# Seven-product down projection, with low parts made by an adding transfer, in a float32 decoder layer on one core

## The chip, the core and the metric

The kernel is one program on one NeuronCore of a Trainium2 chip. The metric is the device time of one execution in microseconds. Engines are named as the profile names them: PE multiplies matrices (PEld is its weight load), DVE and ACT work on vectors, POOL is GpSimd, SP issues the transfers.

## The reference, cut to what matters

The layer ends in a gated MLP. With 512 tokens, 1024 model features and 2816 inner features, the part that is changed is

```
u = causal_dwconv(h @ w_up, ffn_conv_w, ffn_conv_b)      # (512, 5632)
u_gate, u_val = split(u, 2)
x = x + gate_f * ((silu(u_gate) * u_val) @ w_down)       # (512, 2816) @ (2816, 1024)
```

All data are float32. Everything before it (norms, attention, recurrence, merge, output projection) is as it was.

## The kernel before

Features lie on the partitions, tokens along the free axis. A matrix product runs on PE in a rounded type (F32R) that loses low bits, so each float32 operand is kept as two rounded parts, high and low, and `mm3` issues three matmuls per 128x128 block of weights: high by high, high by low, low by high (line 384). `mm` (line 181) is the helper in which every matmul is recorded (L187 in the profile).

Weights come as a stream of chunks of 128x1024, that is eight blocks. A chunk is loaded into one of three `raw` tiles by SP, `split` (line 375) copies it into a `hi` tile on ACT (or, if ACT is behind in the plan, on DVE) and subtracts on DVE into a `lo` tile. There are three of each: a chunk's split waits until PE is done with the chunk three before it, and a load waits until the split of the chunk three before it is done (`stream_to`, `next_chunk`, lines 536 and 548).

The up projection has 44 output tiles of 128 features, one chunk each. For a tile, `conv3` reads the PSUM bank (one ACT and two DVE instructions), and for a pair of tiles `act_task` applies SiLU, multiplies, and splits the product into a pair of rounded slots, `AH[i]` and `AL[i]`; there are 22 of them.

The down projection (lines 1395 to 1407) has 8 output tiles `j`, one after the other, each a sum over the 22 inner tiles `k`. A matmul covers 512 tokens; the last tile goes in two halves of 256. One DVE instruction per tile adds the gated result to the residual `X2[j]`, and SP stores it.

The program is not issued in the order in which it is written. Each operation goes onto a list with a price, and `flush` (line 272) plans it: for each engine it takes, among the next few of its list (`WINDOW`, 160 for PE), the operation that can start first by the planner's own prices, the older one on a tie, and issues it there. The chip's queues then run in exactly this order, whatever the real times are. There is one `flush`, at the end. Tokens' data lie in `pair` tiles (20 slots of 512 columns) and 60 `rslot` tiles.

Of the kernel before, what the change touches and what calls it, by code (L numbers as in the profile page):

```python
# [49 lines left out]
SLACK, NEAR, BACKLOG, LIMIT = 1.2, 2, 8, 2  # L50

FLY, FIRST = 4, 5

# [30 lines left out]
class Emitter:  # L84
# [187 lines left out]
    def flush(self):  # L272
# [23 lines left out]
        end = [None] * len(ops)  # L296
        table = None
# [39 lines left out]
        while left:  # L337
            e = min((x for x in choice if choice[x]), key=lambda x: choice[x][1])
            late, t, i = choice[e]
            op = ops[i]  # L340
            if e == "act" and self.switches(op[5], table):
                t += 1.3
                table = op[5]
            c = pe_cost(t, i) if e == "pe" else op[1]
            free[e] = end[i] = t + c
            if e == "dma":
# [28 lines left out]
    def split(self, hi, lo, x):  # L375

        if self.in_order is None:
            self.act(hi, x, AF.Copy)
        else:
            self.cast(hi.r if isinstance(hi, Buf) else hi, x)  # L380
        h = hi.ap if isinstance(hi, Buf) else hi.bitcast(F32)
        self.tt(lo.r if isinstance(lo, Buf) else lo, x, h, OP.subtract)

    def mm3(self, out, wh, wl, xh, xl, first, last):

# [86 lines left out]
def hybrid_trunk_kernel(ctx: ExitStack, tc: tile.TileContext, xT, vec, cvec, cst, chot, rel, wm, w8, wz, wgate, wbr,  # L472
                        wout, wup, wdn, outT):
    nc = tc.nc
    sb = ctx.enter_context(tc.tile_pool(name="sb", bufs=1))
    pp = ctx.enter_context(tc.tile_pool(name="pp", bufs=1, space=bass.MemoryType.PSUM))
    dr = ctx.enter_context(tc.tile_pool(name="dr", bufs=1, space=bass.MemoryType.DRAM))
    ctx.enter_context(tc.manual_schedule())

    NF, NR = 20, 60  # L480
    slots = []
    for i in range(NF // 2):
        w = sb.tile([128, 1024], F32, name=f"pair{i}")[:]
        slots += [Buf(w[:, :512], w), Buf(w[:, 512:], w)]
    rslots = [Buf(sb.tile([128, 512], F32R, name=f"rslot{i}")[:]) for i in range(NR)]
    banks = [Buf(pp.tile([128, 512], F32, name=f"bank{i}")[:]) for i in range(8)]
    E = Emitter(nc, banks, slots, rslots)
# [6 lines left out]
    halves = (slice(0, 256), slice(256, 512))  # L494
# [21 lines left out]


    c8 = sb.tile([128, 8], F32, name="c8")[:]
    E.dma(c8, cvec, 4, act=True)
    E.dma(CS, cst, 66, act=True)  # L520
    X = [E.slot() for _ in range(KT)]
# [5 lines left out]


    plan = []

    class Stream:
        i = 0
# [3 lines left out]
    def stream_to(n_load, n_split):  # L536
        while Stream.loaded < min(n_load, len(plan)):
            i = Stream.loaded
            src = plan[i]
            E.dma(raws[i % 3][:, :src.shape[-1]], src, 4 * 128 * src.shape[-1] / 1024)  # L540
            Stream.loaded += 1
        while Stream.split < min(n_split, len(plan)):
            i = Stream.split
            n = plan[i].shape[-1]
            E.split(his[i % 3][:, :n], los[i % 3][:, :n], raws[i % 3][:, :n])
# [12 lines left out]

    MODV = sb.tile([128, 32], F32, name="modv")[:]

    def rsqrt(out, ssq, n, inv):

# [43 lines left out]

    ident = CS[:, C_ID:C_ID + 128]
    cp = E.pair()
    gq = sb.tile([128, 2], F32, name="gq")[:]
    relt = sb.tile([32, 16], F32, name="relt")[:]  # L610
    junk = sb.tile([128, 1], F32, name="junk")[:]
    wmp = {}

    def load_wm(f, i):
# [24 lines left out]
    for k in range(KT):  # L639
        t = sq[0 if k == 0 else 3 if k == 7 else 1 + k % 2]  # L640
# [74 lines left out]
    for f in range(KT):  # L715
# [12 lines left out]
        wh, wl = his[f % 3], los[f % 3]  # L728
# [272 lines left out]
    plan.extend(wdn[i] for i in range(22))  # L1001


    mod = {}
# [25 lines left out]
        E.drop(*c2)  # L1030

    nsp = sb.tile([128, 8], F32, name="nsp")[:]

    def nsp_task():
        a, t, s, s2, acc = small(8), small(8), small(8), small(8), small(8)
# [164 lines left out]
    for at, (kind, t) in enumerate(order):  # L1202
# [5 lines left out]
        if kind in ("g", "h"):  # L1208
            b = "g h".index(kind)
# [57 lines left out]
        wh, wl = next_chunk()  # L1267
        z = E.bank()
# [10 lines left out]
    X2 = XR  # L1279
# [83 lines left out]
    def act_task(i, u, w):  # L1363
        yield Need(aps=(u.ap,))
        E.act(u.ap, u.ap, AF.Silu)
        yield Need(aps=(u.ap, w.ap), rslots=2)
        E.tt(u.ap, u.ap, w.ap, OP.mult)
        h, l = E.rslot(), E.rslot()
        E.split(h, l, u.ap)
        E.drop(u, w)  # L1370
        AH.append(h)
        AL.append(l)

    first = []
    E.finish(tn[0])
    for i in range(FIRST):
        wh, wl = next_chunk()
# [1 line left out]
        project(first[i].ap, wh, wl, halves[0], Fh, Fl)  # L1379
    E.finish(tn[1])  # L1380
    E.drop(acc)
    for i in range(44):
# [8 lines left out]
        if i % 2:  # L1391
            ta = E.spawn(act_task(i // 2, uc.pop(i - 1), uc.pop(i)))
    E.finish(ta, t_mod)
    E.drop(*Fh, *Fl)
    dn = []
    for j in range(8):
        for cs in halves if j == 7 else (slice(0, S),):
            z = E.bank()
            for k in range(FT):
                n = j * FT + k  # L1400
                if n // 8 == len(dn):
                    dn.append(next_chunk())
                wh, wl = dn[n // 8]
                E.mm3(z.ap[:, cs], blk(wh, n % 8), blk(wl, n % 8), AH[k].r[:, cs], AL[k].r[:, cs], k == 0, k == FT - 1)
            E.stt(X2[j].ap[:, cs], z.ap[:, cs], mod["gate_f"][:, j:j + 1], X2[j].ap[:, cs], OP.mult, OP.add)
            E.drop(z)
            E.dma(outT[j][:, cs], X2[j].ap[:, cs])
    E.flush()


# [92 lines left out]
```

## Time and profile before

| | |
|---|---|
| three runs, median (lowest to highest) | 904.74 us (904.73 to 904.83) |
| the profiled execution, device time | 904.71 us |
| its span, first to last instruction | 902.9 us |
| PE busy | 893.7 us |
| DVE busy | 629.7 us |
| ACT busy | 473.5 us |
| POOL busy | 1.8 us |
| granted clock of TensorE | 1.000 of full speed |

The span is 1.8 us shorter than the device time; what lies outside it is not in the trace. Matmuls overlap each other in the profile, so the pace of PE is read from the distance between starts and not from the duration of one.

### The profile page before, as it was taken

To read this page: it belongs to the slowest core of one execution; us is meant where nothing else is said; L and a number is where in the kernel's file an instruction comes from. 1 tells how busy PE (TensorE), PEld (TensorE's weight loads), DVE (VectorE), ACT (ScalarE), POOL (GpSimd) and SP (SyncE) were. 2 spreads that over 40 slices of the span, in tenths; PEclk is the share of its full clock that TensorE was granted. 3 is DMA by queue.
4 is the path that set the end of the run, shared out by engine and by line. 5 is a ranking of instruction groups with operands and counts; after the bars stand their busy time and mean duration, and the time that the engine had idled before them with its cause. 6 is when DMAs were issued, how large, how long until landed. Compare 5 with 4: busy or idle time off the path is not lost.

```text
span 902.9 us, 12516 instructions
## 1 busy us (share of the span) xinstructions
PE 893.7 (99%) x4748; PEld 771.9 (85%) x4748; DVE 629.7 (70%) x1131; ACT 473.5 (52%) x759; POOL 1.8 (0%) x15
## 2 busy tenths in 40 slices
PE   7999999999999999999999999999999999999998
PEld 6889989889888888878888999888888888888888
DVE  7989998997876875887676889765666665522321
ACT  5376768985875897732223566544444444321110
POOL 0000000000000000000000000000000000000000
PEclk9999999999999999999999999999999999999999
DMA  9934432452245244685667655333222233333320
GB/s 329 336 117 116 159 82 92 140 159 87 86 160 170 78 144 145 186 289 203 238 230 277 209 184 166 120 106 101 95 94 94 94 98 107 98 117 105 117 82 24
DMA packets 44286, 131.70 MB, mean 146 GB/s; under 512 B 5393, under 2 KB 6937, under 8 KB 44226
## 3 DMA queue, kind: packets, MB, share of 16 engines
q1 hardware_dynamic: 43938, 130.83, 43.6%
q8 instruction: 37, 0.61, 0.3%
q14 instruction: 23, 0.19, 0.1%
q10 hardware_dynamic: 288, 0.07, 0.0%
HBM read 122.46 MB, written 5.80 MB: 142 GB/s over the span
## 4 chain that ended last, share of the span: by engine, by line
PE 93%; ACT 3%; DVE 3%; issue 1%; DMA 0%; POOLq 0%; POOL 0%; DVEq 0%; ACTq 0%
PE bank L187 90%; PE bank L191 2%; ACT pair L213 1%; ACT L213 1%; DVE pair L240 1%; DVE pair L246 0%; DMA c<-in_cvec_dram 0%; DVE pair L243 0%; ACT rslot L213 0%; DVE lo L240 0%; ACT hi L213 0%; DVE rslot L240 0%; DVE pair L258 0%; DVE rslot L243 0%; DVE hi L230 0%
## 5 line engine op out<-in xcount | busy, mean ns | idle before, releaser
L187 PE MATMUL bank<-rslot,hi 128*128 128x512 f32 (+1 forms) x2332 | 657.1, 367 | 0.4 <-ACT rslot L213 0.4
L187 PEld LDWEIGHTS bank<-rslot,hi 128*128 128x128 f32 x2332 | 419.6, 189 | 70.4 <-ACT rslot L213 0.8
L187 PE MATMUL bank<-rslot,lo 128*128 128x512 f32 (+1 forms) x1166 | 427.0, 367 | 0.0
L240 DVE TENSOR_TENSOR lo<-raw,hi 128x1024 fp32r<-128x1024 f32 (+1 forms) x169 | 197.6, 1171 | 151.4 <-ACT hi L213 150.2
L213 ACT ACTIVATE hi<-raw 128x1024 fp32r<-128x1024 f32 (+1 forms) x153 | 156.8, 1025 | 188.5 <-PE bank L187 162.0
L187 PEld LDWEIGHTS bank<-rslot,lo 128*128 128x128 f32 x1166 | 219.8, 189 | 35.7
L187 PE MATMUL bank<-hi,rslot 128*128 128x256 f32 (+1 forms) x448 | 92.0, 315 | 0.3 <-ACT rslot L213 0.3
L243 DVE SCALAR_TENSOR_TENSOR pair<-bank,V,pair 128x511 f32<-128x511 f32 (+2 forms) x112 | 83.5, 746 | 2.8 <-ACT pair L213 1.1
L187 PEld LDWEIGHTS bank<-hi,rslot 128*128 128x128 f32 x448 | 74.3, 190 | 6.6 <-issue 0.9
L213 ACT ACTIVATE rslot<-pair 128x512 fp32r<-128x512 f32 (+2 forms) x60 | 37.2, 622 | 75.8 <-DVE pair L240 71.7
L246 DVE CUSTOM_DVE_ANT_0 pair<-pair,pair,V 128x1024 f32<-128x1024 f32 x48 | 61.1, 1278 | 10.8 <-DMA pair<-in_wm_dram 10.8
L213 ACT ACTIVATE pair<-bank,V 128x512 f32<-128x512 f32 (+1 forms) x84 | 61.6, 733 | 4.7 <-PE bank L187 4.0
L213 ACT ACTIVATE pair<-bank 128x512 f32<-128x512 f32 (+3 forms) x76 | 43.3, 604 | 39.1 <-PE bank L187 38.6
L187 PE MATMUL bank<-lo,rslot 128*128 128x256 f32 (+1 forms) x224 | 62.5, 315 | 0.0
L213 ACT ACTIVATE pair<-pair 128x512 f32<-128x512 f32 (+1 forms) x59 | 33.5, 569 | 46.1 <-DVE pair L243 44.8
L240 DVE TENSOR_TENSOR rslot<-pair,rslot 128x512 fp32r<-128x512 f32 (+2 forms) x67 | 45.4, 679 | 15.1 <-ACT rslot L213 14.7
L240 DVE TENSOR_TENSOR pair<-pair,pair 128x512 f32<-128x512 f32 (+1 forms) x72 | 45.6, 635 | 13.2 <-ACT pair L213 8.3
L213 ACT ACT_TABLE_LOAD x37 | 47.5, 1283 | 6.1 <-PE bank L187 3.8
L187 PE MATMUL bank<-rslot,rslot 128*128 128x256 f32 (+3 forms) x288 | 48.7, 309 | 0.0
L187 PEld LDWEIGHTS bank<-rslot,rslot 128*128 128x128 f32 x288 | 43.4, 189 | 4.7 <-DVE rslot L240 0.8
L213 ACT ACTIVATE pair<-pair,small 128x256 f32<-128x256 f32 (+3 forms) x78 | 40.4, 528 | 10.5 <-DVE small L234 9.4
L187 PEld LDWEIGHTS bank<-lo,rslot 128*128 128x128 f32 x224 | 42.7, 190 | 2.6
(79 smaller groups left out, 410.3 us busy)
## 6 DMA issues: line engine op xcount, KB each, us to landing
raw<-in_wz_dram SPq DMA_DIRECT2D x50, 512.0 KB, 3.4
raw<-in_wup_dram SPq DMA_DIRECT2D x49, 512.0 KB, 3.3
pair<-in_wm_dram SPq DMA_DIRECT2D x48, 512.0 KB, 5.0
raw<-in_wdn_dram SPq DMA_DIRECT2D x22, 512.0 KB, 3.3
raw<-in_wout_dram SPq DMA_DIRECT2D x16, 512.0 KB, 3.3
pair<-in_xT_dram SPq DMA_DIRECT2D x16, 256.0 KB, 5.0
raw<-in_w_dram SPq DMA_DIRECT2D x8, 512.0 KB, 6.1
raw<-in_wbr_dram SPq DMA_DIRECT2D x16, 256.0 KB, 3.0
```

Source lines behind the costliest of these rows:

```text
L187: self._go("pe", cost, [out], [lhsT, rhs], lambda: self.nc.tensor.matmul(out, lhsT, rhs, start=start, stop=stop), rows=lhsT.shape[0] / 128)
L191: self._go("pe", 0.107, [out], [in_, ident], lambda: self.nc.tensor.transpose(out, in_, ident))
L213: self._go("act", c, outs, ins, lambda: self.nc.scalar.activation(out, in_, func, scale=scale, **kw), "tanh" if func == AF.Tanh else t)
L240: self._dve([out], [a, b], lambda: self.nc.vector.tensor_tensor(out, a, b, op=op))
L243: self._dve([out], [a, s, b], lambda: self.nc.vector.scalar_tensor_tensor(out, a, s, b, op0=op0, op1=op1))
L246: self._dve([out, accum], [a, b, s], lambda: self.nc.vector.tensor_tensor_reduce(out, a, b, 1.0, s, op0, op1, accum_out=accum))
```

## The change

Output tiles go in four pairs. The first pair is computed as before, but both tiles side by side, in chunks of four inner tiles. For each of the other three pairs, the first 14 of the 22 inner tiles go as seven pairs of inner tiles by Strassen's scheme: a 2x2 block product (two output tiles, two inner tiles, two halves of the tokens) by seven products of 256 tokens in place of eight. The remaining 8 inner tiles go as before, in two chunks.

The sums of weight blocks are made by three DVE additions per chunk ahead of its split, which then covers 896 columns; the four differences of activations per pair of inner tiles are made by DVE in `act_task`, stored to DRAM, and read back, split and kept as `TH`, `TL` during the first pair of output tiles. To have room, the residual is stored to DRAM during the up projection, the plan is flushed ahead of the down projection, and the pool of `pair` tiles is closed and a smaller one opened in its place. For the two plain chunks of each of the three pairs the low part is not subtracted on DVE: ACT writes the high part and its negative, and a transfer issued by POOL adds the raw chunk onto the latter. The planner prices that transfer at 4.0 us from issue to use.

```
+    def split_add(self, hi, lo, x):
+        self.act(hi, x, AF.Copy)
+        self.act(lo, hi.bitcast(F32), AF.Copy, scale=-1.0)
+        self._go("pool", 1.0, [lo], [x], lambda: self.nc.gpsimd.dma_start(lo, x, accum_op=OP.add), table=4.0)
...
             if i in sevens:
+                E.tt(w[:, 512:768].rearrange("p (a n) -> p a n", a=2), w[:, None, 0:128].to_broadcast([128, 2, 128]),
+                     w[:, 128:384].rearrange("p (a n) -> p a n", a=2), OP.add)
+                E.tt(w[:, 768:896], w[:, 512:640], w[:, 256:384], OP.add)
+                E.tt(w[:, 896:1024], w[:, 768:896], w[:, 384:512], OP.add)
+                w = w[:, 128:]
...
+            (E.split_add if i in added else E.split)(his[i % 3][:, :n], los[i % 3][:, :n], w)
...
+        E.tt(t4[0], e.ap[:, a], e.ap[:, b], OP.subtract)
+        E.stt(t4[1], t4[0], -1.0, u.ap[:, b], OP.mult, OP.subtract)
+        E.tt(t4[2], u.ap[:, b], e.ap[:, b], OP.subtract)
+        E.stt(t4[3], t4[1], -1.0, u.ap[:, a], OP.mult, OP.subtract)
+        E.dma(d_t[i // 2], t[0].whole, 512)
...
+    E.flush()
+    first_pool.close()
+    E.slots = take_slots(zp, 8, "z")
...
+        def plain():
+            zs = [E.bank() for _ in range(3 if jp == 3 else 2)]
+            for ks in rest if jp else every:
+                wh, wl = next_chunk()
...
+                for (j, z, cs), k in seq:
+                    n = j * len(ks) + k - ks.start
+                    E.mm3(zs[z].ap[:, cs], blk(wh, n), blk(wl, n), AH[k].r[:, cs], AL[k].r[:, cs], k == (2 * SEVEN if jp else 0),
+                          k == FT - 1)
...
+        def seven():
+            b = [E.bank() for _ in range(4)]
+            for q in range(SEVEN):
+                wh, wl = next_chunk()
...
+                for n, x, cs, z, zc in ((1, e, a, 0, a), (2, o, a, 1, a), (6, o, c, 1, c), (5, t[1], None, 0, c),
+                                        (3, t[0], None, 2, a), (4, t[2], None, 2, c), (0, t[3], None, 3, a)):
+                    E.mm3(b[z].ap[:, zc], blk(wh, n), blk(wl, n), xh, xl, f, l)
+            y, y2, u, w = E.slot(), E.slot(), E.slot(), E.slot()
+            E.act(y.ap[:, a], b[0].ap[:, a], AF.Copy)
+            E.act(w.ap[:, c], b[2].ap[:, a], AF.Copy)
+            E.tt(u.ap[:, a], y.ap[:, a], b[0].ap[:, c], OP.add)
+            E.tt(w.ap[:, a], u.ap[:, a], b[2].ap[:, c], OP.add)
+            E.tt(y.ap[:, c], u.ap[:, a], w.ap[:, c], OP.add)
+            E.tt(y.ap, y.ap, b[1].ap, OP.add)
+            E.stt(xs[0].ap, y.ap, mod["gate_f"][:, j0:j0 + 1], xs[0].ap, OP.mult, OP.add)
+            E.tt(y2.ap[:, a], w.ap[:, a], b[3].ap[:, a], OP.add)
+            E.tt(y2.ap[:, c], w.ap[:, a], w.ap[:, c], OP.add)
+            E.stt(xs[1].ap, y2.ap, ngate[:, j1:j1 + 1], xs[1].ap, OP.mult, OP.add)
...
+        if jp == 0:
+            t_combos = E.spawn(combos())
+            out = plain()
+            E.finish(t_combos)
+        else:
+            seven()
+            out = plain()
```

In the last pair the plain part of its second tile goes in halves of 256, as the last tile did before.

## Rows read from the trace of the kernel before

**Rows 1.** The page, part 1: busy us (share of span), instructions.

```profile
PE 893.7 (99%) x4748; PEld 771.9 (85%) x4748; DVE 629.7 (70%) x1131; ACT 473.5 (52%) x759; POOL 1.8 (0%) x15
```

**Rows 2.** The chain that ended last, 770 us on: start, us, what.

```profile
769.90 129.86 PE bank L187 x635
899.76 0.02 issue
```

**Rows 3.** Groups by form, 779.2 us on: busy us, mean ns, idle before, releaser.

```profile
L187 PE MATMUL bank<-rslot,hi 128*128 128x512 f32 x308 | 94.9, 389 | 0.0
...
L187 PE MATMUL bank<-rslot,lo 128*128 128x512 f32 x154 | 59.9, 389 | 0.0
...
L240 DVE TENSOR_TENSOR lo<-raw,hi 128x1024 fp32r<-128x1024 f32 x20 | 24.5, 1226 | 66.3 <-ACT hi L213 66.2
L213 ACT ACTIVATE hi<-raw 128x1024 fp32r<-128x1024 f32 x20 | 21.2, 1061 | 80.1 <-PE bank L187 80.1
L187 PE MATMUL bank<-rslot,hi 128*128 128x256 f32 x88 | 15.9, 283 | 0.0
L187 PE MATMUL bank<-rslot,lo 128*128 128x256 f32 x44 | 12.4, 283 | 0.0
L243 DVE SCALAR_TENSOR_TENSOR pair<-bank,modv,pair 128x512 f32<-128x512 f32 x7 | 5.2, 749 | 8.6 <-PE bank L187 8.6
```

**Rows 4.** Timeline of PE near 800 us: start, us.

```profile
800.57 0.39 PE L187 MATMUL bank<-rslot,lo 128*128 128x512 f32 x1
...
801.25 0.39 PE L187 MATMUL bank<-rslot,lo 128*128 128x512 f32 x1
```

**Rows 5.** The same near 886 us, in the last tile.

```profile
886.15 0.28 PE L187 MATMUL bank<-rslot,lo 128*128 128x256 f32 x1
...
886.51 0.28 PE L187 MATMUL bank<-rslot,lo 128*128 128x256 f32 x1
```

**Rows 6.** Windows: length, PE, PEld, DVE, ACT, POOL busy, PEclk, DMA, GB/s.

```profile
650.00:700.00 50.00, 50.00 (x222) 41.39 (x222) 31.68 (x39) 21.40 (x28) 0.00 (x0) 1.00 0.29 95
810.00:850.00 40.00, 40.00 (x179) 33.10 (x178) 10.00 (x9) 7.70 (x8) 0.00 (x0) 1.00 0.37 123
```

**Rows 7.** Groups of DVE by form, whole span.

```profile
L230 DVE CAST hi<-raw 128x1024 fp32r<-128x1024 f32 x12 | 8.3, 688 | 8.0 <-PE bank L187 7.9
...
L240 DVE TENSOR_TENSOR pair<-pair,pair 128x256 f32<-128x256 f32 x14 | 5.7, 414 | 0.0
...
L240 DVE TENSOR_TENSOR rslot<-bank,rslot 128x128 fp32r<-128x128 f32 x16 | 3.8, 280 | 0.6 <-ACT rslot L213 0.6
```

**Rows 8.** The page, part 6: transfers, KB each, median us to landing.

```profile
raw<-in_wdn_dram SPq DMA_DIRECT2D x22, 512.0 KB, 3.3
...
raw<-in_w_dram SPq DMA_DIRECT2D x8, 512.0 KB, 6.1
raw<-in_wbr_dram SPq DMA_DIRECT2D x16, 256.0 KB, 3.0
```

**Rows 9.** One tile, raw, 560 to 800 us: its loads' durations in ns, landing.

```profile
L267 SPq DMA_DIRECT2D raw<-in_wdn_dram x9: 327/328/328, 754.2 to 797.7; - x9
...
DMA to landing us min/median/max: 3.2/3.3/4.5
```

**Rows 10.** Timeline where up ends and down begins.

```profile
779.01 1.06 ACT L213 ACTIVATE hi<-raw 128x1024 fp32r<-128x1024 f32 x1 [0.95 <-PE bank L187]
...
784.20 0.69 DVE L240 TENSOR_TENSOR rslot<-pair,rslot 128x512 fp32r<-128x512 f32 x1 [0.70 <-ACT rslot L213]
```

**Rows 11.** Timeline of the end.

```profile
899.78 0.48 DVE L243 SCALAR_TENSOR_TENSOR pair<-bank,modv,pair 128x256 f32<-128x256 f32 x1 [7.43 <-PE bank L187]
900.29 0.33 SPq L267 DMA_DIRECT2D out_dram<-pair  x1
```

More of the change, by code (lines that the diff above doesn't have):

```diff
@@ L345, in flush @@
             free[e] = end[i] = t + c
+            if e == "pool" and op[5]:
+                end[i] = t + op[5]
             if e == "dma":
@@ L480, in hybrid_trunk_kernel, with take_slots @@
     NF, NR = 20, 60
[L481 to L484, printed above, removed]
+    def take_slots(pool, n, tag=""):
+        out = []
+        for i in range(n // 2):
+            w = pool.tile([128, 1024], F32, name=f"pair{tag}{i}")[:]
+            out += [Buf(w[:, :512], w), Buf(w[:, 512:], w)]
+        return out
     rslots = [Buf(sb.tile([128, 512], F32R, name=f"rslot{i}")[:]) for i in range(NR)]
     banks = [Buf(pp.tile([128, 512], F32, name=f"bank{i}")[:]) for i in range(8)]
-    E = Emitter(nc, banks, slots, rslots)
+    E = Emitter(nc, banks, [], rslots)
     raws = [sb.tile([128, 1024], F32, name=f"raw{i}")[:] for i in range(3)]
@@ L518, in hybrid_trunk_kernel @@
     c8 = sb.tile([128, 8], F32, name="c8")[:]
+    MODV = sb.tile([128, 32], F32, name="modv")[:]
+    gq = sb.tile([128, 2], F32, name="gq")[:]
+    relt = sb.tile([32, 16], F32, name="relt")[:]
+    junk = sb.tile([128, 1], F32, name="junk")[:]
+    nsp = sb.tile([128, 8], F32, name="nsp")[:]
+    ngate = sb.tile([128, 8], F32, name="ngate")[:]
+    first_pool = ExitStack()
+    E.slots = take_slots(first_pool.enter_context(tc.tile_pool(name="px", bufs=1)), NF)
     E.dma(c8, cvec, 4, act=True)
@@ L529, in hybrid_trunk_kernel @@
     plan = []
+    sevens, added = set(), set()
     class Stream:
@@ L539, in stream_to @@
             src = plan[i]
-            E.dma(raws[i % 3][:, :src.shape[-1]], src, 4 * 128 * src.shape[-1] / 1024)
+            for c, p in [(0, src)] if not isinstance(src, list) else src:
+                E.dma(raws[i % 3][:, c:c + p.shape[-1]], p, 4 * 128 * p.shape[-1] / 1024)
             Stream.loaded += 1
@@ L1000, in hybrid_trunk_kernel, with blocks @@
     plan.extend(wup[i] for i in range(44))
-    plan.extend(wdn[i] for i in range(22))
+    def blocks(js, ks):
+        out = []
+        ns = [j * FT + k for j in js for k in ks]
+        at = 0
+        while at < len(ns):
+            e = at + 1
+            while e < len(ns) and ns[e] == ns[e - 1] + 1 and ns[e] % 8:
+                e += 1
+            c = ns[at] % 8 * 128
+            out.append((at * 128, wdn[ns[at] // 8][:, c:c + 128 * (e - at)]))
+            at = e
+        return out
+    every, rest = [[range(k, min(k + 4, FT)) for k in range(k0, FT, 4)] for k0 in (0, 2 * SEVEN)]
+    plan.extend(blocks((0, 1), ks) for ks in every)
+    for jp in range(1, 4):
+        js = (2 * jp, 2 * jp + 1)
+        sevens.update(range(len(plan), len(plan) + SEVEN))
+        plan.extend(blocks(js[::-1], (2 * q, 2 * q + 1)) for q in range(SEVEN))
+        added.update(range(len(plan), len(plan) + len(rest)))
+        plan.extend(blocks(js, ks) for ks in rest)
     mod = {}
@@ L1369, in act_task @@
         E.split(h, l, u.ap)
-        E.drop(u, w)
+        E.drop(w)
         AH.append(h)
         AL.append(l)
+        if i >= 2 * SEVEN:
+            E.drop(u)
+            return
+        if i % 2 == 0:
+            kept[i] = u
+            return
+        yield Need(pairs=1)
+        t = E.pair()
+        e, t4 = kept.pop(i - 1), [t[j // 2].ap[:, halves[j % 2]] for j in range(4)]
+        a, b = halves
+        E.tt(t4[0], e.ap[:, a], e.ap[:, b], OP.subtract)
+        E.stt(t4[1], t4[0], -1.0, u.ap[:, b], OP.mult, OP.subtract)
+        E.tt(t4[2], u.ap[:, b], e.ap[:, b], OP.subtract)
+        E.stt(t4[3], t4[1], -1.0, u.ap[:, a], OP.mult, OP.subtract)
+        E.drop(e, u)
+        E.dma(d_t[i // 2], t[0].whole, 512)
+        E.drop(*t)
     first = []
+    d_x = [dr.tile([128, S], F32, name=f"dx{k}")[:] for k in range(KT)]
+    d_t = [dr.tile([128, 1024], F32, name=f"dt{q}")[:] for q in range(SEVEN)]
     E.finish(tn[0])
@@ L1381, in hybrid_trunk_kernel @@
     E.drop(acc)
+    kept = {}
     for i in range(44):
@@ L1394, in hybrid_trunk_kernel @@
     E.drop(*Fh, *Fl)
[L1395 to L1407, printed above, removed]
+    E.ts(ngate, mod["gate_f"], -1.0, None, OP.mult)
@@ new lines, in hybrid_trunk_kernel, with combos @@
+    E.flush()
+    first_pool.close()
+    E.ops, E.in_order = [], 0
+    zp = ctx.enter_context(tc.tile_pool(name="pz", bufs=1))
+    E.slots = take_slots(zp, 8, "z")
+    more = max(0, 4 * SEVEN - len(E.rslots))
+    E.rslots += [Buf(zp.tile([128, 512], F32R, name=f"rslotz{i}")[:]) for i in range(more)]
+    TH, TL = [], []
+    def combos():
+        for q in range(SEVEN):
+            yield Need(pairs=1)
+            t = E.pair()
+            E.dma(t[0].whole, d_t[q], 512)
+            yield Need(aps=(t[0].whole,))
+            h, l = [E.rslot(), E.rslot()], [E.rslot(), E.rslot()]
+            for i in range(2):
+                E.split(h[i], l[i], t[i].ap)
+            E.drop(*t)
+            TH.append([h[j // 2].r[:, halves[j % 2]] for j in range(4)])
+            TL.append([l[j // 2].r[:, halves[j % 2]] for j in range(4)])
```

43 lines of the change are left out of this document (36 added, 7 removed).

## The prediction

> **What bounds the kernel now.** I read the page's busy shares first. PE is busy for 99% of the span, and no other engine comes near [rows 1]. Busy time of overlapping matmuls proves little, so the next view is the chain of waits in order of time: from 769.90 us to 899.76 us it is PE alone, 635 matmuls with no wait between them [rows 2]. So in this stage a microsecond taken from PE is a microsecond of the kernel, as long as nobody makes PE wait. What remains is the price of a matmul. From start to start, three matmuls of 512 columns take 801.25 - 800.57 = 0.68 us, 0.2267 each [rows 4]; three of 256 take 0.36 us, 0.120 each [rows 5]. Half the columns cost 53%, not 50%: each matmul carries about 0.013 us that does not shrink. The down projection has 308 + 154 = 462 of the first kind and 88 + 44 = 132 of the second [rows 3], so 462 x 0.2267 + 132 x 0.120 = 120.6 us, and 899.76 - 120.6 = 779.2 is where the timeline shows the up projection ending [rows 10]. The sum closes without any idle time.
>
> **What the seven products save on PE.** One pair of inner tiles for two output tiles costs 2 x 2 x 3 = 12 matmuls of 512, 2.72 us. Seven products cost 7 x 3 = 21 matmuls of 256, 2.52 us. Eight to seven is 12.5%, but 7.4% is left, because there are nearly twice as many matmuls. For the second and third pair of output tiles: before 132 x 0.2267 = 29.92; after 147 x 0.120 + 48 x 0.2267 = 17.64 + 10.88 = 28.52; 1.40 saved each. The last pair already had 132 of its matmuls at 256: before 66 x 0.2267 + 15.84 = 30.80; after 17.64 + 24 x 0.2267 + 48 x 0.120 = 28.84; 1.96 saved. The first pair costs the same. Sum: 2 x 1.40 + 1.96 = **4.76 us saved**, 0.53%. This is a ceiling; nothing else on PE goes away.
>
> The fixed part per matmul is where a rule and the trace part. The Trainium skill, page "TensorE: Matmul & The Clock Gate", section "Back-to-back issue gap", puts the gap at the columns at full clock plus 2.5 ns; that would be 0.2158 and 0.1092 us here, and the saving an estimated 6.3 us. The rows show 13 ns and not 2.5, so the sum stays with the rows.
>
> **Work that is added, and its cover.** In the up projection 28 subtractions of 256 columns at 0.414 us [rows 7] add 11.6 us to DVE over 28 chunks (152 us). DVE has 18 us free in every 50 there, and transfers keep the DMA engines busy for 0.29 of it [rows 6]; the stores (7 of 512 KB, 8 of 256 KB) fit too. PE waits for none of it, since the weights' splits run two chunks ahead. Nothing. If that cover were gone, a late split would cost PE as much as it is late.
>
> During the first pair of output tiles DVE and ACT split fourteen activation halves: 14 x 0.69 = 9.7 us of DVE [rows 10] in 29.9 us where DVE is busy a quarter [rows 6]. The loads are 7 x 512 KB, on SP between the chunks. Nothing: needed only afterwards.
>
> The closed pool: SP's first loads of the new phase wait for the last user of the old slots, at 784.20 + 0.69 = 784.9, 5.7 us after the last up matmul [rows 10]. Behind them on SP stands the fourth chunk, which PE wants only after 3 x 5.44 = 16.3 us. Nothing.
>
> In the seven-product chunks the split waits for PE as it does now (ACT idles 80.1 us of this stage for PE [rows 3]). Per chunk DVE does 0.414 + 2 x 0.280 [rows 7] and the low part of 896 columns, 7/8 of 1.226 = 1.07 [rows 3]: 2.05 us against PE's 2.52. From PE's release to the finished split ACT's 0.93 and DVE's 1.07 with hand-overs make 2.3 us, and two chunks (5.04) are there for it. The longest loop is that of a raw tile: two issues of 0.33 [rows 9], landing 3.0 for a load of at most 256 KB [rows 8], additions 1.0, cast 0.93, subtraction 1.07, hand-overs 0.4, in all some 6.7 us against 3 x 2.52 = 7.56. Nothing, with 0.9 us to spare, and the first three chunks of each run of seven have their splits or loads done during the plain chunks ahead.
>
> The epilogue of the seven products is five DVE instructions of 256 columns, one of 0.69 and two of 0.75 [rows 3, 7, 10]: 4.3 us beside 10.9 us of plain chunks. Nothing.
>
> At the end, three stores follow each other within 3 us where one stood alone [rows 11]; I put 0.2 us on it, between 0 and one issue of 0.33.
>
> **The adding transfer.** This is the one price that no row shows. Let 0 be the end of the fifth seven-product chunk; its `hi` tile then goes to the first plain chunk. ACT casts (1.06) and writes the negative (1.06) [rows 3], with hand-overs POOL issues at 2.65. PE has two more chunks of seven products, to 5.04. The order on PE is fixed by the planner: by its own prices the low part is usable 2.0 us after PE gets to the plain chunk, so it puts about ten matmuls of the high part first. On the chip the first low matmul therefore stands at 5.04 + 10 x 0.2267 = 7.31, and the transfer has 7.31 - 2.65 = **4.7 us** from issue to use. Beyond that PE stands still, one for one, once per pair, three times in all. The second plain chunk is kinder: issued at 5.15, needed at 10.93, 5.8 us. Behind the waiting transfer POOL has only the next one, behind the waiting matmul PE has the rest of the chunk; the raw tile is held until it is read, and its next load is wanted some 10 us later.
>
> Bounds: a plain load of the same 512 KB lands after 3.3 us [rows 8], below which it will not come. It must read two operands, so two such transfers one behind the other, 6.6, is the other end; the 6.1 us of a load among busy DMA engines [rows 8] lies just inside. From 256 to 512 KB a load grows by only 0.3 us [rows 8], so doubled reading alone would give some 3.9, and POOL's issue comes on top of that. I take the middle, 5.0: 0.3 us of standstill each, 0.9 in all. The ends give 0 and 3 x 1.9 = 5.7 us. (The Trainium skill, "DMA: Bandwidth & Descriptors", section "Anatomy of one DMA", has 2.0 us and the bytes at 436 GB/s for a GpSimd transfer; with both operands read that is an estimated 4.4 us, no standstill, 900.1. No run here shows it yet.)
>
> **Sum.** 904.71 - 4.76 + 0.9 + 0.2 = 901.05 for the profiled execution; the median lies 0.03 above it, so **901.1 us**.
>
> **Rivals.** What a measurement can tell from no change is about 0.2%, 1.8 us: 902.9 to 906.5 counts as the same.
>
> *The transfer is late, somewhat.* Between 5.6 and 6.8 us from issue to use, each pair loses 0.9 to 2.1 us, and the time is 902.9 to 906.5: the saving is eaten. For it speak the 6.1 us row; against it, that few loads run beside it (0.37 busy [rows 6]).
>
> *The transfer is very late, and the kernel slower.* The place is the tenth matmul of the first plain chunk of each of the three pairs, the price three times what the transfer takes beyond 4.7 us, and it decides from 6.8 us on; at 8 us the time is 910. It would need POOL's issue to cost microseconds, or the addition to halve the rate. The trace has no transfer from POOL to rule it out. As a mechanism of this kernel: where the planner gives a cast to DVE, which it did 12 times at 0.688 us [rows 7], a busy DVE could hold up POOL's issue; one such cast per transfer would cost 3 x 0.7 = 2.1 us, 903.2. The Trainium skill, "SBUF — State Buffer", section "Who interferes with whom", says so: such a copy on DVE shuts GpSimd out of a shared port while it builds a transfer. From 779 us on the trace has no cast on DVE [rows 3], so I give that little weight.
>
> *The load loop sets the pace.* If loads land in 4.5 us, the longest of [rows 9], the raw loop is 8.2 us, 0.2 us per chunk too long, 21 chunks: 4.5 us, 905.5, the same. It would stand in the waits as PE waiting for ACT or DVE within the seven-product chunks. Against it: the median is 3.3, and each run has three chunks of lead.
>
> *Closing the pool stops everyone.* If PE too waits for the last user of the old slots, that is 5.7 us once: 906.8. Against it, PE reads none of the new tiles for 30 us.
>
> **How the numbers follow.** Forecast, with the transfer under 5.6 us: 0.60, 900.1 to 902.9, the likeliest 901.1. Somewhat late: 0.16. Load loop: 0.06. Very late: 0.13. Pool: 0.05. Faster 0.60, the same 0.16 + 0.06 = 0.22, slower 0.13 + 0.05 = 0.18. The range runs from 900.0, just under no standstill at all, up to the end of the somewhat late case, 906.5, which leaves out the last two.
>
> **What would show it.** Right: starts of the seven products' matmuls 0.120 us apart; the down projection 116 to 117 us long; PE waiting at three places only, about 2.3 us into each first plain chunk, for the POOL transfer, under 1 us each; 5 us from POOL's issue to landing. Wrong: a longer pitch (at 0.1295 the second and third pair save nothing), PE waiting inside the runs of seven, a gap at 779 us, or waits for POOL of 2 us and more.

## The result, and the profile after

The changed kernel takes 921.32 us (median of 4 runs, 921.19 to 922.75) against 904.79 for the kernel before in the same comparison: a ratio of 1.0184, interval 1.0171 to 1.0197. It is 16.5 us slower, where 901.1 had been forecast with 906.5 as the upper end. In its profiled execution it took 922.75 us with a span of 920.6.

For the medians below one thing has to be known: some executions, of the kernel before too (906.0 in place of 904.6), are some 1.4 us longer, and in the four profiled ones of that kind the granted clock is 0.50 for 3.4 us at the program's start where the others have 1.00, as in these windows of two of the experiments (pieces with the later plan, then all three edits; length, busy PE, PEld, DVE, ACT, POOL, granted clock, DMA share, GB/s).

```profile
13.00:16.41 3.41, 3.41 (x17) 3.41 (x18) 2.14 (x10) 1.32 (x2) 0.00 (x0) 0.50 1.01 335
...
13.00:16.41 3.41, 3.41 (x33) 3.41 (x32) 3.08 (x13) 2.03 (x4) 0.00 (x0) 1.00 0.97 338
```

The page of the changed kernel, part 1 (busy us), part 4 (share of the chain that ended last) and part 6 (transfers):

```profile
PE 897.0 (97%) x4895; PEld 778.6 (85%) x4895; DVE 681.3 (74%) x1266; ACT 498.2 (54%) x796; POOL 7.0 (1%) x21
...
PE 81%; DMA 6%; DVE 5%; ACT 4%; issue 3%; SPq 0%; ACTq 0%; POOL 0%; DVEq 0%; POOLq 0%
...
raw<-in_wdn_dram SPq DMA_DIRECT2D x56, 128.0 KB, 2.8
```

PE is busy for 97% of the span and no longer for 99% [rows 1], and the loads of the last matrix went from 22 of 512 KB [rows 8] to 72: the 56 of 128 KB shown, and 16 of 256 KB. Where before one line of PE ran to the end [rows 2], the chain is now in pieces; this is the chain of the changed kernel from 700 us on:

```profile
699.87 79.35 PE bank L189 x350
...
785.09 6.52 DMA pairz<-dt
...
796.15 6.12 DMA pairz<-dt
...
832.21 6.04 DMA lo<-raw
...
862.17 3.34 DMA raw<-in_wdn_dram
865.57 4.24 issue
869.82 4.58 DMA lo<-raw
874.44 17.29 PE bank L189 x83
...
901.94 4.50 DMA lo<-raw
906.49 10.56 PE bank L189 x66
```

The combination loads of the first pair of output tiles stand in it, and after them the three adding transfers, one for each of the other pairs. Between 862 and 874 us the chain is a load, 4.24 us that the view calls "issue" (a copy and two casts stand there in order on ACT) and a transfer, and nothing of it is PE. To put numbers on the stages I took the distance from the first matmul of each pair of output tiles to that of the next (in the profiled executions, counting matmuls off in PE's order; the prediction's own figures in the first line):

| us | pair 1 | pair 2 | pair 3 | pair 4 |
|---|---|---|---|---|
| predicted without standstill | 29.92 | 28.52 | 28.52 | 28.84 |
| changed kernel | 33.99 | 37.01 | 36.38 | 30.45 |

Sum of the losses: 4.07 + 8.49 + 7.86 + 1.61 = 22.0 us. In pairs 2 and 3 most of it lies in one chunk, the first plain one, which takes 11.43 and 12.81 us where 24 matmuls of 0.2267 make 5.44. POOL's issues in the changed kernel:

```profile
832.21 1.00 POOL L392 DMA_DIRECT2D lo<-raw  x1 [449.99 <-ACT lo L215]
838.01 0.86 POOL L392 DMA_DIRECT2D lo<-raw  x1 [4.80 <-DVE raw L242]
869.82 0.86 POOL L392 DMA_DIRECT2D lo<-raw  x1 [30.95 <-ACT lo L215]
...
901.94 0.86 POOL L392 DMA_DIRECT2D lo<-raw  x1 [29.23 <-ACT lo L215]
```

and the matmuls at the first of them, from PE's timeline:

```profile
838.30 1.04 PE L189 MATMUL bank<-rslot,lo 128*128 128x512 f32 x2 [4.03 <-DMA lo<-raw]
839.13 1.05 PE L189 MATMUL bank<-rslot,hi 128*128 128x512 f32 x2
839.99 0.63 PE L189 MATMUL bank<-rslot,lo 128*128 128x512 f32 x1
```

The fifth seven-product chunk ended at 827.42, and POOL issued 4.8 us later, not 2.65. The transfer landed after 6.0 us, and PE started nothing from 833.87 to 838.30 (waits of PE are told here from start to start). What comes after the wait is slow too: (839.99 - 838.30) / 4 = 0.42 us per matmul and not 0.2267. In pair 3 PE waited from 868.98 to 873.37, and once more until the transfer landed at 874.40:

```profile
868.18 1.20 PE L189 MATMUL bank<-rslot,hi 128*128 128x512 f32 x4 [0.34 <-ACT hi L215]
873.37 0.80 PE L189 MATMUL bank<-rslot,hi 128*128 128x256 f32 x2 [3.99 <-ACT hi L215]
874.44 1.22 PE L189 MATMUL bank<-rslot,lo 128*128 128x512 f32 x2 [0.28 <-DMA lo<-raw]
```

The long one of these two ends with a cast on ACT and not with the transfer: the plan had put two matmuls of pair 4's first seven-product chunk ahead of the first low one, and that chunk's cast was late. The transfer, which landed 1.0 us after it, would have held PE nearly as long. The windows around the two long waits (columns as above):

```profile
838.30:841.80 3.50, 3.50 (x9) 2.71 (x10) 1.09 (x1) 0.50 (x1) 0.57 (x1) 0.53 0.70 151
842.20:845.00 2.80, 2.80 (x14) 2.27 (x13) 0.00 (x0) 0.00 (x0) 0.00 (x0) 1.00 0.98 268
...
873.40:879.40 6.00, 5.72 (x14) 4.37 (x15) 1.04 (x1) 0.00 (x0) 0.00 (x0) 0.50 0.97 228
```

After each wait of 4.4 us the granted clock is at its lower level, 1.2 GHz, for 3.5 and 6 us, in which matmuls take nearly twice as long: some 1.8 and 3.0 us on top of the waits. What the splits waited for, by the waits from 770 us on (us in total, times, longest):

```profile
ACT hi L215 <- DVE raw L242: 44.7, 12, 8.9
...
DVE raw L242 <- DMA raw<-in_wdn_dram: 16.1, 6, 6.7
...
ACT rslotz L215 <- DMA pairz<-dt: 7.8, 1, 7.8
```

Before, ACT waited for PE there and for no load [rows 3]. So the loads had become late, and SP's own timeline at the start of the phase shows in which order it issued them:

```profile
784.61 0.43 SPq L269 DMA_DIRECT2D raw<-in_wdn_dram  x1
785.09 1.38 SPq L269 DMA_DIRECT2D pairz<-dt  x3
786.51 2.46 SPq L269 DMA_DIRECT2D raw<-in_wdn_dram  x3
793.67 0.33 SPq L269 DMA_DIRECT2D pairz<-dt  x1
```

One piece of a chunk is issued, then three transfers of 512 KB whose result PE wants only from the second pair on (813 us), then the chunk's next pieces.

### The profile page after: what moved, and what is told of

It is laid out like the page before. It is cut to its first block, busy times and chain, and to the rows that moved or that the text cites. A ratio compares the mean times of both kernels' runs of the same rounds, so it can differ in the third digit from the quotient of the medians.

```text
span 920.6 us, 13209 instructions
## 1 busy us (share of the span) xinstructions
PE 897.0 (97%) x4895; PEld 778.6 (85%) x4895; DVE 681.3 (74%) x1266; ACT 498.2 (54%) x796; POOL 7.0 (1%) x21
## 4 chain that ended last, share of the span: by engine, by line
PE 81%; DMA 6%; DVE 5%; ACT 4%; issue 3%; SPq 0%; ACTq 0%; POOL 0%; DVEq 0%; POOLq 0%
PE bank L189 79%; DMA raw<-in_wdn_dram 2%; PE bank L193 2%; DMA lo<-raw 2%; ACT pair L215 1%; DMA pairz<-dt 1%; ACT hi L215 1%; ACT L215 1%; DVE lo L242 1%; DVE raw L242 1%; DVE pair L242 1%; DVE pair L245 0%; SPq L269 0%; DVE rslotz L242 0%; DVE pair L248 0%
## 5 line engine op out<-in xcount | busy, mean ns | idle before, releaser
L189 PE MATMUL bank<-rslot,hi 128*128 128x512 f32 (+1 forms) x2358 | 646.6, 362 | 6.6 <-ACT hi L215 6.2
L242 DVE TENSOR_TENSOR lo<-raw,hi 128x1024 fp32r<-128x1024 f32 (+2 forms) x174 | 200.9, 1157 | 97.7 <-ACT hi L215 96.4
L189 PEld LDWEIGHTS bank<-rslot,lo 128*128 128x128 f32 x1179 | 222.9, 190 | 43.7 <-DMA lo<-raw 6.4
L215 ACT ACTIVATE hi<-raw 128x1024 fp32r<-128x1024 f32 (+2 forms) x164 | 165.5, 1013 | 167.5 <-PE bank L189 91.4
```

Source lines behind the costliest of these rows:

```text
L189: self._go("pe", cost, [out], [lhsT, rhs], lambda: self.nc.tensor.matmul(out, lhsT, rhs, start=start, stop=stop), rows=lhsT.shape[0] / 128)
L215: self._go("act", c, outs, ins, lambda: self.nc.scalar.activation(out, in_, func, scale=scale, **kw), "tanh" if func == AF.Tanh else t)
L242: self._dve([out], [a, b], lambda: self.nc.vector.tensor_tensor(out, a, b, op=op))
```

## The experiments

Three suspects stood out: the adding transfer; the pieces in which a chunk is loaded (two to four where a chunk was one load); and the second plan, which begins with all queues free at its time 0, while on the chip SP's first load of the phase can't go before the old slots are free. The edits take them away one at a time and together.

**No transfer: DVE subtracts, as for all other chunks.**

```
-        added.update(range(len(plan), len(plan) + len(rest)))
```

> The changed kernel, but the low parts of the six plain chunks are subtracted on DVE as all others are; no transfer is issued by POOL. Theory A (the adding transfer, issued late, makes PE stand and its clock fall): the three first plain chunks, which took 11.4, 12.8 and 7.0 us, come near 5.4, 5.4 and 5.6; some 13 us less, 908 us in all, with the granted clock at full. Theory B (the loads and splits of the seven-product chunks run late, and the transfer only shows it): the cast stays late, DVE's subtraction takes the transfer's place in the wait, and less than 5 us come back, above 916 us.

905.67 us (904.2 to 907.76, 10 runs), ratio 1.0011 (1.0001 to 1.0021). The pairs take 32.55, 30.00, 28.54 and 28.91 us, the first plain chunks 5.5. This is theory A, and more than its 13 us: the transfer costs 15.65 us as the kernel stands. Without it 2.6 us of loss remain in pair 1 and 1.5 in pair 2.

**Second plan: transfers start 8 us later.**

```
-    def flush(self):
+    def flush(self, dma_from=0.0):
...
-        moved = 0.0
+        moved = dma_from
+        free["dma"] = dma_from
...
-    E.flush()
+    E.flush(dma_from=8.0)
```

> The changed kernel, but the second plan is told that no transfer can start in its first 8 us, so that it puts the splits of the activation differences, which wait for late loads, behind the fourth and fifth weight chunk's on ACT and DVE. Theory A (the first pair's 34.0 us against 29.9 are ACT standing in order for those loads): about 4 us less, 917 us. Theory C (the DMA engines, full from 790 to 800 us, make the weights themselves late): the first pair stays at 33 us or more, 920 us or above.

920.02 us (919.43 to 923.68), 1.0175 (1.0154 to 1.0196); pairs 36.35, 36.09, 34.70, 30.21. Only 1.3 us, which the two intervals do not tell from nothing, and the time of theory C: that the plan's early start alone made the loads late falls. The reason that theory C gives, full DMA engines, is taken up with the pieces planned as one, below. (The profiled execution is 3.7 us above the median, so its pairs are on the long side.)

**One load per chunk.** The weights are laid out so that every chunk is contiguous (512 columns for a seven-product chunk, 1024 for a plain one).

```
-        plan.extend(blocks(js[::-1], (2 * q, 2 * q + 1)) for q in range(SEVEN))
+        plan.extend(wds[(jp - 1) * SEVEN + q] for q in range(SEVEN))
...
-        plan.extend(blocks(js, ks) for ks in rest)
+        plan.extend(wdn[len(every) + (jp - 1) * len(rest) + i] for i in range(len(rest)))
...
```

> The changed kernel, but the weights of the down projection are laid out so that each chunk is one transfer in place of two to four. POOL's adding transfers stay. Theory B (late loads set the pace): the casts of the first plain chunks come earlier in the second and third pair, the waits for the transfer shrink from 4.2 us to the 1.2 us of the last pair, the clock does not fall; 8 to 12 us less, 909 to 913 us. Theory A without B: the transfer takes 4.5 to 6 us anyway, at most 3 us come back, 918 us or above.

909.38 us (908.48 to 911.78), 1.0053 (1.0037 to 1.0069); pairs 29.92, 34.49, 30.33, 30.18. This is the range of theory B. Pair 1 is whole. In pair 2 a new order on DVE shows: an addition that waits for its load, at 811.97, stands ahead of the subtraction that PE wants, at 812.96.

**All three edits.**

> All three edits together: low parts on DVE, the second plan's transfers from 8 us on, one transfer per chunk. What then is left is the seven products themselves. If the sum of matmuls by their pace holds and nobody else is in the way, the saving of 4.8 us comes out: 900 to 901 us. If DVE (2.05 us of work per chunk of seven products in 2.52) is in the way, PE waits inside the runs of seven and the time stays at 903 us or above.

900.16 us (899.98 to 900.39), 0.9947 (0.9932 to 0.9962); pairs 29.92, 28.54, 28.54, 28.88. Its chain from 760 us on:

```profile
759.95 135.16 PE bank L189 x826
895.11 0.02 issue
895.13 0.48 DVE pairz L245
```

PE alone again, as in [rows 2], and 4.6 us sooner. The pairs are the predicted ones to 0.04 us.

**The transfer back, the other two edits kept.**

> As the run with all three edits (900.16 us), but the low parts of the plain chunks come by POOL's adding transfer again. It prices the transfer by itself, with loads on time. Theory A (even on time it costs the 1.3 to 2.1 us per pair that were left with one load per chunk): 904 to 905.5 us. Theory B (with the loads on time it is hidden): 900 to 901 us.

904.76 us (904.18 to 906.9, 10 runs), 1.0004 (0.9994 to 1.0013); pairs 29.92, 30.69, 29.01, 30.61. Here the loads are on time, and this is the case that the prediction had worked out. At the first transfer, the timeline of that kernel, PE:

```profile
826.58 1.10 PE L189 MATMUL bank<-rslot,hi 128*128 128x512 f32 x4
829.51 0.73 PE L189 MATMUL bank<-rslot,lo 128*128 128x512 f32 x2 [1.84 <-DMA lo<-raw]
```

and POOL:

```profile
824.13 0.99 POOL L393 DMA_DIRECT2D lo<-raw  x1 [441.92 <-ACT lo L215]
```

The fifth seven-product chunk ends at 821.54 and POOL issues at 824.13, 2.59 us later: 2.65 was predicted. The landing (4.6 to 5.3) is about the predicted 5.0. But only four high matmuls of the chunk stand ahead of the first low one, not ten, so PE waits 2.2 us here (the other two waits: 0.55 in pair 3, where four matmuls of the next run of seven stand there too, and 1.34 in pair 4, where its three banks let six go first, four of them of 256 columns), and the transfer costs 904.76 - 900.16 = 4.6 us.

**A dearer price of the transfer in the plan, 6.0 in place of 4.0 us** (on the kernel just shown). If the price decides how many high matmuls go first, a higher one should move more of them ahead.

> The run before with one number changed: the planner prices the adding transfer at 6.0 us in place of 4.0, so that it puts more matmuls of the high part ahead of the first that needs the low part. If what is left of the cost is the order on PE, it goes down to 901 to 902 us; if the plan has no more high matmuls to put there or the transfer is later still, it stays within 1 us of the run before.

905.07 us (903.65 to 907.59, 10 runs), 1.0002 (0.9993 to 1.0012). Still the same number of high matmuls of the chunk. What the dearer price does move is four more matmuls of the next run of seven, in pair 3 alone (twelve in place of eight before the first low one), and the wait there is gone; waits of 1.9 and 1.3 us stay in pairs 2 and 4. The price isn't what limits the chunk's own.

**High matmuls listed first** (on the kernel with the transfer back): in the first plain chunk all high matmuls come on the list ahead of the low ones.

```
+                for (j, z, cs), k in seq if jp and not last else ():
+                    n = j * len(ks) + k - ks.start
+                    E.mm(zs[z].ap[:, cs], blk(wh, n), AH[k].r[:, cs], k == 2 * SEVEN, False)
+                    E.mm(zs[z].ap[:, cs], blk(wh, n), AL[k].r[:, cs], False, False)
...
```

> As the run with the transfer put back (904.76 us), but in the list each first plain chunk of the last three pairs has all its matmuls of the high part ahead of all of the low part. Theory: the plan keeps the matmuls into one bank in the list's order, so that with two banks only four high matmuls can go ahead of the first low one, whatever the transfer's price; with sixteen ahead PE gets there 16 x 0.227 = 3.6 us after the chunk's start, the transfer has 5.0 + 3.6 - 2.6 = 6.0 us, takes 4.6 to 5.3, and is hidden: 900.2 to 900.8 us. Rival: the order is not it, as the dearer price changed nothing: 904 us or above.

900.55 us (900.42 to 901.74), 0.9951 (0.9938 to 0.9965); pairs 29.92, 28.65, 28.54, 28.90, landing 4.5 to 5.1. The transfer is as long as before and costs nothing that the intervals can tell. Its chain:

```profile
759.79 135.51 PE bank L189 x827
895.30 0.03 issue
```

What held the order, by the planner's code, was the bank: `mm3` puts three matmuls into one bank in a row, the planner keeps writes to one bank in the list's order, and with two banks it gets past two low matmuls only, each with two high ones ahead of it.

**The same order alone, on the changed kernel.**

> The changed kernel (921.3 us) with that same order of the list as its only edit: loads in pieces, second plan from 0. Theory: 12 x 0.227 = 2.7 us of each wait (4.2, 4.2 and 1.2 us) are covered, what remains is too short for the clock to fall, and the 4.8 us at half clock come back too: 2.7 + 2.7 + 1.2 + 4.8 = 11.4 us less, 910 us. Rival: the late casts of these chunks take the high matmuls with them, and less than 6 us come back, 915 us or above.

919.8 us (916.93 to 920.27), 1.015 (1.0133 to 1.0168); pairs 33.92, 29.31, 37.74, 33.47. The rival's time, and a miss for the theory: only 1.5 us. Pair 2 gets 7.7 us back, pairs 3 and 4 lose 4.4 together, with new waits in other places (2.9 us at 851, 1.9 at 862, 2.1 at 877), landings of up to 6.4 us, and the granted clock at 0.50 for 3.4 us from 880.04 after the last of these waits. With loads late, mending one order moves the waits on.

**No seven products** (`SEVEN = 0`; all else as with all three edits; the down projection is done wholly in plain chunks).

> As the run with all three edits, but no pair of inner tiles goes by seven products: all chunks of all four pairs are plain, subtracted on DVE, with nothing stored or read back of activation differences. It leaves the second plan, the closed pool, the residual's way through DRAM and the tiles side by side. If these cost nothing, 904.8 us, as before the change, and the 4.6 us are the seven products' alone; if they cost something, it stands above by that.

904.92 us (904.86 to 905.25, 10 runs), 0.9998 (0.9989 to 1.0008); pairs 29.92, 29.92, 29.92, 30.94, no gap on PE. The second plan, the closed pool and the pairing of output tiles cost nothing by themselves, and 904.92 - 900.16 = 4.76 us is what the seven products save; the sums of the pairs, 120.70 and 115.88, say 4.82.

**Plan from 0 again, one load per chunk, no transfer.**

> Low parts on DVE and one transfer per chunk, but the second plan lets its transfers start at once. If the later start is needed on top of the single loads, the 4.0 us that PE waited at the second chunk of the first run of seven (5.4 us in place of 2.5, and 0.8 and 0.3 beside it) come back and the time is 904 us; if not, 900 to 901 us.

904.97 us (902.26 to 905.64, 10 runs), 0.9993 (0.9983 to 1.0003); pairs 29.96, 33.53, 28.54, 28.88. The first three seven-product chunks take 3.91, 5.73 and 2.91 us, all others 2.52. In the trace the order on DVE of the run with one load per chunk is there again, an addition that waits for its load ahead of the subtraction that PE wants:

```profile
812.96 1.08 DVE L242 TENSOR_TENSOR raw<-raw 128x256 f32<-128x256 f32 x3 [2.56 <-DMA raw<-in_wds_dram]
813.95 1.08 DVE L242 TENSOR_TENSOR lo<-raw,hi 128x896 fp32r<-128x896 f32 x1
```

PE waits 1.4 and 2.1 us for it (until 810.45 and 815.09), and after that the granted clock is at its lower level for 3.4 us:

```profile
812.95:815.09 2.14, 0.28 (x3) 0.07 (x1) 2.06 (x5) 0.89 (x1) 0.00 (x0) 1.00 0.00 0
816.05:819.47 3.42, 3.42 (x19) 3.42 (x18) 2.86 (x6) 0.37 (x1) 0.00 (x0) 0.50 0.77 213
```

Of the 5.0 us that pair 2 loses, an estimated 1.7 (half of the stretch) are the clock.

**Pieces, plan from 8 us, no transfer.**

> As the run with all three edits (900.16 us), but the weights of the down projection come in two to four transfers per chunk again. If the single transfers are what brings the first pair to 29.9 us and the runs of seven to their pace, the first pair loses 2.6 us and the first run of seven 1.5 us again, as with the low parts on DVE alone: 904 us or above. If the subtraction on DVE and the later start are enough, 900 to 901 us.

905.28 us (902.97 to 905.97, 10 runs), 1.0000 (0.9990 to 1.0009); pairs 34.00, 28.54, 28.54, 28.90. The pieces cost 4.1 us, all of it in pair 1, though pair 1 is computed from chunks as large as before. The median says 5.1, as most executions of this kernel are of the kind that is 1.4 us longer, the profiled one among them.

**Pieces, but planned as one operation.** The planner knows a `raw` tile under one name, so a chunk's second piece is to it another write of the same tile, which may be issued only when it reckons the first to have landed; and in between it issues something else. Here one planned operation issues all pieces one behind the other. First with plan from 8 us and no transfer, then alone on the changed kernel.

```
-            for c, p in [(0, src)] if not isinstance(src, list) else src:
-                E.dma(raws[i % 3][:, c:c + p.shape[-1]], p, 4 * 128 * p.shape[-1] / 1024)
+            ps = [(0, src)] if not isinstance(src, list) else src
+            outs = [raws[i % 3][:, c:c + p.shape[-1]] for c, p in ps]
+            E._go("dma", 0.5 * sum(p.shape[-1] for _, p in ps) / 370, outs[:1], [p for _, p in ps],
+                  lambda outs=outs, ps=ps: [nc.sync.dma_start(o, p) for o, (_, p) in zip(outs, ps)])
+            E.w[raws[i % 3].tensor.name] += 2.0
```

> Low parts on DVE, the second plan's transfers from 8 us on, and the pieces of each chunk planned as one operation. Theory as above: 900.2 to 900.8 us, as with the weights laid out for one transfer. Rival: the first pair keeps its 34.0 us, as with pieces planned singly, 904 us or above.

899.97 us (899.87 to 900.21), 0.9946 (0.9929 to 0.9963); pairs 29.92, 28.54, 28.54, 28.88. The same pieces over the same queue are as good as single loads once the plan treats them as one. Its SP timeline at the start of the phase:

```profile
784.52 0.90 SPq L569 DMA_DIRECT2D raw<-in_wdn_dram  x2
785.47 1.38 SPq L269 DMA_DIRECT2D pairz<-dt  x3
786.89 6.66 SPq L569 DMA_DIRECT2D raw<-in_wdn_dram  x7
794.35 2.34 SPq L269 DMA_DIRECT2D pairz<-dt  x3
```

Both pieces of the first chunk go ahead of the combination loads, and seven pieces follow before the next combination load, where the changed kernel had three. The pieces of 128 KB don't land sooner for it between 779 and 800 us (count, size, median us to landing, in this run and then with the pieces planned singly):

```profile
raw<-in_wdn_dram SPq DMA_DIRECT2D x10, 128.0 KB, 6.5
...
raw<-in_wdn_dram SPq DMA_DIRECT2D x5, 128.0 KB, 4.7
```

Pair 1 is whole with 6.5 us and loses 4.1 with 4.7, so it is the time of issue that counts, and not, as theory C had it, how long full DMA engines take.

> The changed kernel with its two to four transfers per chunk, but planned as one operation, so that they are issued one behind the other. Theory: the planner keeps track of a raw tile as a whole, takes a second piece for a second write of the same tile, and issues it only when it reckons the first one landed, 2.4 to 3.3 us later; that, and not the pieces, made the loads late. Then the time comes to that of one transfer per chunk, 909 us. Rival: pieces with short rows are slow in themselves: less than 4 us come back, 917 us or above.

914.02 us (912.33 to 914.95), 1.0099 (1.0084 to 1.0114), between the two expectations. Pair 1 is whole (29.92) and pairs 3 and 4 lose only what the transfer costs in its order (30.32, 30.17). Pair 2 takes 38.77, 4.3 us more than with one load per chunk: its first and second chunks take 4.75 and 8.33 us, each counted up to the first matmul of the next. The chain there is loads:

```profile
809.06 0.44 DVE raw L242
810.05 1.09 DVE lo L242
811.17 0.33 SPq L568
811.55 3.88 DMA raw<-in_wdn_dram
815.54 0.43 DVE raw L242
```

The early plan is still in this kernel, and its cost in pair 2 is larger with pieces than without. An estimated 1.2 of the 4.3 us are the clock: it is 0.50 for 6.8 us from 816.59, with PE busy for 5.74 of them, against 3.41 us, all of them busy, from 815.61 with one load per chunk, and half of the difference is lost. The rest wasn't tried further.

**An eighth feature pair, `SEVEN = 8`** (on the kernel with all three edits, with six slots in the new pool in place of eight).

> As the run with all three edits (900.16 us), with eight of eleven pairs of inner tiles by seven products, and six token slots in place of eight in the second phase to make room. By the pace of the matmuls each pair of inner tiles saves 2.72 - 2.52 = 0.20 us three times: 899.6 us. If the fewer slots or the eighth set of activation differences makes somebody wait, 900.2 us or above.

900.68 us (899.45 to 902.1, 5 runs), 0.9951 (0.9938 to 0.9963); pairs 29.92, 29.33, 28.34, 28.60. Pairs 3 and 4 gain 0.20 and 0.28 us as the pace says, but pair 2 stands 1.0 us for the two further combinations, whose loads end its chain (`pairz<-dt`, 5.67 us at 807.70). No better than seven.

Together, what each set of suspects costs over the 900.16 us without any, by the medians, and by the sum of the four pairs in the profiled execution over the 115.88 us of that run:

| left in the kernel | median, us | cost, us | in the pairs, us |
|---|---|---|---|
| transfer | 904.76 | 4.6 | 4.4 |
| early plan | 904.97 | 4.8 | 5.0 |
| pieces | 905.28 | 5.1 | 4.1 |
| pieces, early plan | 905.67 | 5.5 | 4.1 |
| transfer, early plan | 909.38 | 9.2 | 9.0 |
| transfer, pieces | 920.02 | 19.9 | 21.5 |
| all three | 921.32 | 21.2 | 22.0 |

Each alone eats about the whole saving of 4.76. Pieces and early plan together cost no more than one of them. Transfer and pieces together cost 10.2 us more than their sum. As the traces read, a late piece makes the cast late, the cast makes POOL's issue late, the wait on PE grows to 4.4 us with a lower clock behind it, and the raw tile, held until the transfer has read it, makes the next loads late; no run takes these links apart. In the profiled execution of that kernel the granted clock is 0.50 for 13.7 us after 800 us, and with the transfer alone or the pieces alone (both with the later plan) it stays at 1.00 there.

## Why the prediction was wrong, step by step

**The saving on PE: right.** 4.76 us predicted, 4.76 measured between the kernels with and without the seven products; that they agree to the last digit is luck, as each median is good to some 0.1 us. (The rule of the Trainium skill, page "TensorE: Matmul & The Clock Gate", section "Back-to-back issue gap", gave an estimated 6.3. That section of the Trainium skill states the rule for a matmul by itself and says that in a stream of weight loads and matmuls both set the spacing; here each matmul has a weight load of its own, and the trace's 13 ns per matmul decide.) The changed kernel's own pitch in a run of seven is the one of [rows 5]: three matmuls in 826.58 - 826.22 = 0.36 us.

```profile
826.22 0.28 PE L189 MATMUL bank<-rslot,lo 128*128 128x256 f32 x1
...
826.58 0.28 PE L189 MATMUL bank<-rslot,lo 128*128 128x256 f32 x1
```

**"The loads are 7 x 512 KB, on SP between the chunks. Nothing: needed only afterwards": failed, 4.1 us.** I took it that a chunk's loads go out together and that combination loads fit between chunks. The plan puts them between the pieces of one chunk.

**"The longest loop is that of a raw tile ... 6.7 us against 7.56 ... Nothing": failed as a step.** The sum of the loop took the two issues as back to back, 2 x 0.33. In the plan the second waits for the first to be reckoned landed. Its terms were also added up wrongly: 0.66 + 3.0 + 1.0 + 0.93 + 1.07 + 0.4 is 7.06 us and not 6.7, which leaves 0.5 us to spare and not 0.9, and makes the rival's loop 8.6 us and its price 7 us. The rival "the load loop sets the pace" named the place but not the mechanism (landings of 4.5 us) and priced it at 4.5 us; in the run of seven of pair 2 the changed kernel loses 2.5 us of PE time by it and in that of pair 3 0.5. The much larger part came out elsewhere, as a late cast ahead of the transfer.

**"POOL issues at 2.65": right only with loads on time.** 2.59 with the loads on time; 4.8 and 7.2 in pairs 2 and 3 of the changed kernel. In pair 3 the chunk's own load began only at 862.17 and took until 865.5, against 862.64 for the end of the fifth chunk, and ACT's copy of the seven products' bank also stands ahead of the cast. The sum took the split's inputs as ready.

**"It puts about ten matmuls of the high part first": failed.** Four of the chunk's own; the budget from issue to use was 4.7 - 6 x 0.2267 = 3.3 us and not 4.7. I had worked out the order from the planner's prices and left out that it keeps writes to one bank in order. With loads on time this alone makes the 0.9 us of the sum 4.6, inside the rival "the transfer is late, somewhat" (902.9 to 906.5) though its reason was a longer transfer.

**The transfer's own time, 5.0: right.** 4.5 to 6.1 us in the changed kernel, 4.6 to 5.3 with the loads on time. (The Trainium skill's "DMA: Bandwidth & Descriptors", section "Anatomy of one DMA", gave an estimated 4.4; the quickest here took 4.5.) No row had priced it, and 5.0 was the middle between two bounds, so that it fits is in part luck; why some took 6 us isn't shown. The 921 us lie where the rival "very late" put them, but not by its mechanism: POOL was busy for 0.86 to 1.00 us per issue, DVE has no cast in this stage, and it was the issue that came late, by 2.1 us and more after the predicted 2.65 in pairs 2 and 3.

**The closed pool: nothing, as predicted** by 904.92 with it and no seven products. But the same closing brought the second plan with its start at 0, 4.8 us by itself (some 1.7 of it the lower clock), which I had not costed at all: I looked at what waits for the pool and not at what a new plan believes about the queues.

**The end, 0.2 us: right.** 900.16 against 904.76 - 4.76 leaves 0.16, about what the medians can tell.

**The clock** was in no step. It was at its lower level after two waits of 4.4 us and took some 4.8 us of the 22.

Of the signs named ahead, the pitch came out right; PE waiting inside the runs of seven, and waits for POOL of 2 us and more, were the signs of a wrong forecast, and both stand in the trace.

The error was of one kind. The prices were right, of matmuls, transfer and pool. The three orders that carry the 21 us, of a chunk's pieces, of the second plan's loads and of high and low matmuls, I had from what the code means to do and not from the rules by which the planner orders it. Four versions beat both kernels: pieces planned as one without transfer and with the later plan, 899.97 us; all three edits, 900.16; the transfer with the high matmuls listed first, 900.55; and eight pairs, 900.68.

## What to carry to other kernels

In a kernel whose queues run in a planned order, read first what the planner holds to be dependent (a tile under one name, a bank, a queue that it thinks free), since an operation whose duration is hidden can still cost the whole gain by where it is put. Price delays that meet in one chain together: here two of 4 to 5 us each made 20. Before giving up on a slow operation, try to give it more room; with the loads on time, 5 us of transfer were free as soon as sixteen matmuls, not four, stood ahead of its use.

## What the runs showed of the hardware

- After waits of 4.4 us in an otherwise full stretch TensorE's granted clock was 0.53 and 0.50 of full speed for 3.5 and 6 us. After waits of 2.1 to 2.3 us both came: it stayed at 1.00 in the kernel with the transfer back (wait until 829.51), and was 0.50 for 3.4 us, from 815.61 and 816.05, in the kernels with one load per chunk (wait until 814.10) and with the plan from 0 again (until 815.09). What decides between the two isn't shown here.
- An adding transfer of 512 KB from one tile to another landed 4.5 to 6.4 us after POOL's issue (48 transfers in eight kernels), of which POOL itself was busy 0.86 to 1.0.
- Loads cut into pieces, most of 128 KB (rows of 1 KB) in place of one contiguous load, cost no measurable time in this kernel when issued one behind the other: 899.97 us with them, 900.16 with single loads.
